# A two-layer retention, convolution and mixture-of-experts step: weight ring placed first in SBUF, other end order, token counts copied by ScalarE

## The chip, the cores and the metric

One core of a Trainium2 chip runs the whole program in one launch. The metric is the device time of one execution in microseconds (us), the median of several runs. All data is float32.

## The reference, cut to what matters

128 context tokens and 128 latent tokens pass two layers. Layer 0 mixes tokens by retention, layer 1 by a short gated convolution. After each mixer comes a layer norm and a mixture of 64 experts, of which each token uses six, and then another norm, whose result is the layer's output:

```python
x = layer_norm(DEEPNORM_ALPHA * x + g1 * y, ln_g[i, 0], ln_b[i, 0])
h = x * (1 + sc2) + sh2
y = moe_ffn(h, router_w, router_bias, w_gate, w_up, w_down, ...)
x = layer_norm(DEEPNORM_ALPHA * x + g2 * y, ln_g[i, 1], ln_b[i, 1])
```

An expert is `(silu(t @ w_gate) * (t @ w_up)) @ w_down` with weights of 1024x256, 1024x256 and 256x1024, 3 MB in all. Sixty-four experts in two layers are some 400 MB, most of what the program reads.

## The kernel before, in words

**Weights.** Every large weight passes through one SBUF tile, the ring (L37): 14 slots of 2048 floats (8 KB) per partition, 1 MB each. `plan` fixes the order of the units for the whole program; `Stream.pump` (L48) issues the next unit's DMAs on the SP queue as soon as the unit 14 places earlier is marked used (`done`), and the framework makes SP wait until the engines that read that slot are through. A gate/up unit is two DMAs of 512 KB with 4 KB per partition each (`u_gu`, L223), a down unit one of 1 MB with 8 KB per partition (`u_down`, L231). The units of the last block are loaded in column halves (`u_last`, L235): the left halves of all four experts, then the right halves.

**SBUF.** Pools are laid out in the order in which they are opened: constants (`const`), then the ring, then working tiles. In the program of before the first constant, x, lies at byte 4,224 of each partition, and the ring begins at byte 17,440, which is 34 x 512 + 32. Every ring slot is a multiple of 512 bytes long, so every slot begins 32 bytes past such a multiple.

**Routing.** `router` and `router_turn` make the scores, `route` (L1131) picks the experts. From the chosen mask (L1149) TensorE counts tokens into two PSUM banks (L1153 to L1159): `bk` holds each token's rank in its expert, `cnt` the tokens of each expert, once along the free axis (128x64) and once along the partitions (64x1). Then six small matmuls run that only keep TensorE's clock up (`warm`, L131). VectorE goes on in this order: ranks (L1164, reads `bk`), the slot tables `P0` (`slots`, L1273, four instructions), the low halves of the split activations `L` (L1169, two of 128x1024), the combine weights (L1172 to L1176), the copy of the counts out of `cnt` (L1181), sort keys (L1182, L1183; the latter reads `cnt` again), the order of the experts (L1184 to L1188).

**Gathering.** `moe` then calls `gather_first` (L1307): 32 matmuls into all four rotating PSUM banks 0 to 3, first the 16 with the high halves `H`, then 8 with `L` of the context tokens and 8 with `L` of the latent ones; inside each group bank 0 comes first and bank 3 last. `cnt` lies in one of these four banks. ScalarE copies the result to SBUF (L1316), and the first block's gate and up products (L1351) follow.

**Experts.** 24 blocks per layer (`pair`, L1406): eight of two experts, four of four, eight of two, four of four. A block multiplies gate and up in four parts (L1351), takes silu and product, turns the result (L1366), multiplies by the down weights of the block before (`down`, L1371), whose result ScalarE and VectorE split into `hi` and `lo` (L1381, L1382), and adds it to the accumulators (`combine`, L1386, matmuls of L121). VectorE takes the accumulators into the norm (`ln_part`, L982).

**The end.** In the last block (L1430 to L1446) TensorE does: down of block 22 left and right, down of block 23 left, combine of block 22 left and right, combine of block 23 left, down of block 23 right, its combine. `ln2_out` (L1541) scales and stores four tiles of 128x512: three by VectorE (L1554, L1555) and one, the right half of the context tokens, by ScalarE (L1550) and GpSimd (L1551, L1552); each goes out by a DMA of 256 KB (L1556).

`Y`, a tile of 8 KB per partition, holds the scaled norm weights first (read by GpSimd, L1002 and L1003) and later the `hi` and `lo` of every second block (L1381).

Of the kernel before, what the change touches and what calls it, by code (L numbers as in the profile page):

```python
# [7 lines left out]
F32 = mybir.dt.float32  # L8
# [3 lines left out]
AF = mybir.ActivationFunctionType  # L12
OP = mybir.AluOpType
# [4 lines left out]
NT = 2  # L18
NEXP = 64
# [52 lines left out]
class Kernel:  # L72
    WN = (12, 4, 14, 6, 22)

    def __init__(self, ctx, tc, I, O, dbg=None, nblocks=4 * len(TABLES), layers=2):
        self.ctx, self.tc, self.nc, self.I, self.O = ctx, tc, tc.nc, I, O
        self.dbg = dbg or {}
        self.nb, self.layers = nblocks, layers
        self.const = ctx.enter_context(tc.tile_pool(name="const", bufs=1))
        self.ring = ctx.enter_context(tc.tile_pool(name="ring", bufs=1))  # L80
        self.work = ctx.enter_context(tc.tile_pool(name="work", bufs=1))
        self.dram = ctx.enter_context(tc.tile_pool(name="dram", bufs=1, space=bass.MemoryType.DRAM))
        self.psum = ctx.enter_context(tc.tile_pool(name="psum", bufs=1, space=bass.MemoryType.PSUM))
        self.st = Stream(self.nc, self.ring)
        self.nm = 0
        self.pj = 0
        self.adabank = self.rtbank
        self.rt = 0
# [271 lines left out]
    def setup(self):  # L360
        nc, I, const = self.nc, self.I, self.const
        self.x = const.tile([128, NT, D], F32, name="x")
        self.cc = const.tile([128, NT, KD], F32, name="cc")
        self.st.pump(1)
        self.dummy = const.tile([128, 1], F32, name="dummy")
        self.mhalf = const.tile([128, 2], F32, name="mhalf")
        nc.gpsimd.memset(self.mhalf, -0.5)
        self.table(AF.Silu)
        self.cp = const.tile([128, 257], F32, name="cp")
        self.dl = const.tile([128, 8], F32, name="dl")  # L370
        self.t6 = self.w([128, 2 + 2 * KD + 128], F32, "T6")
        self.start_rows = self.t6[0:2 * KD, 2 + 2 * KD:]
        nc.scalar.dma_start(out=self.cp, in_=I["cst_id"])
        nc.scalar.dma_start(out=self.dl, in_=I["ret_decay"].rearrange("a d h -> a (d h)").to_broadcast([128, 8]))
        nc.sync.dma_start(out=self.cc[:, 0], in_=I["c_ctx"].rearrange("(p k) -> p k", k=KD))
        nc.sync.dma_start(out=self.cc[:, 1], in_=I["c"][0].rearrange("(p k) -> p k", k=KD))
        nc.scalar.dma_start(out=self.start_rows, in_=I["ada_b"][0, 0:2048].rearrange("(r p) -> r p", p=128))
        self.load_x()
        self.st.pump()

        self.ident, self.iota, self.part = self.cp[:, 0:128], self.cp[:, 128:256], self.cp[:, 256:257]
        self.cs = const.tile([128, 2 * KD + 32], F32, name="cs")
        nc.gpsimd.memset(self.cs, 0.0)

        self.one = const.tile([128, 3], F32, name="one")
        nc.gpsimd.memset(self.one, 0.0)
        nc.gpsimd.memset(self.one[64:128, 0:1], 1.0)
        nc.gpsimd.memset(self.one[0:64, 2:3], 1.0)
        self.gse = const.tile([128, NT, 12], F32, name="gse")
        nc.gpsimd.memset(self.gse, SENT)  # L390
        self.onesb = const.tile([128, 128], BF16, name="onesb")
        nc.gpsimd.memset(self.onesb, 1.0)
        self.trib = const.tile([128, 128], BF16, name="trib")

        self.tie = const.tile([128, NEXP + 1], F32, name="tie")
        self.rb = const.tile([128, NEXP], F32, name="rb")

        self.lnr = const.tile([128, 512], F32, name="lnr")
        nc.gpsimd.memset(self.lnr, 0.0)

        self.ab = const.tile([128, 2, KD, NT], F32, name="ab")
        self.b1, self.a1 = self.ab[:, 0], self.ab[:, 1]
        nc.scalar.activation(self.cs[:, 0:2 * KD].rearrange("p (k t) -> p k t", t=2), self.cc.rearrange("p t k -> p k t"),
                             AF.Silu)

        self.ident2 = const.tile([128, 64], F32, name="ident2")
        nc.vector.tensor_add(self.ident2, self.ident[:, 0:64], self.ident[:, 64:128])
# [413 lines left out]
    def retention(self):  # L821
        nc, U, st = self.nc, self.U, self.st
        qb, kb, bks = self.start()
        prev = None
        for h in range(4):
# [16 lines left out]
            if prev:  # L842
                z = self.ret_head_z(*prev)
# [29 lines left out]
            for d in range(2):  # L873
# [3 lines left out]
                                               op0=OP.mult, op1=OP.subtract)  # L877
            v[1] = self.w([128, 2, 512], F32R, "T6")
            if h == 1:
                for t in range(NT):  # L880
                    nc.gpsimd.tensor_scalar(self.x[:, t], self.x[:, t], ALPHA, 1.0, op0=OP.mult, op1=OP.mult)
                self.new_acc()
            if h == 2:
                for x, y in ((self.tie[:, 0:NEXP], self.iota[:, 0:NEXP]), (self.tie[:, NEXP:NEXP + 1], self.part)):
                    nc.vector.tensor_scalar(x, y, FIXED + 0.5, -2.0 ** 20, op0=OP.is_lt, op1=OP.mult)
                    nc.vector.tensor_add(x, x, y)
# [244 lines left out]
    def route(self, l):  # L1131
        nc = self.nc
# [24 lines left out]
            nc.tensor.matmul(cnt[:, 0:64], self.onesb, maskb[:, t], start=(t == 0), stop=(t == 1))  # L1157
        for t in range(NT):
            nc.tensor.matmul(cnt[0:64, 64:65], maskb[:, t], self.onesb[:, 0:1], start=(t == 0), stop=(t == 1))  # L1159
        self.warm(6)  # L1160
        V.tensor_scalar(mask, res[:, :, 0:64], HIT_T, None, op0=OP.is_ge)
        rc = self.rc = self.w([128, 2, NT, NEXP], F32, "rc")
# [11 lines left out]
        V.reciprocal(ws, ws)  # L1174
        for t in range(NT):
            V.tensor_scalar(self.comb[:, t], self.comb[:, t], ws[:, t:t + 1], 2.5, op0=OP.mult, op1=OP.mult)  # L1176

        self.od = od = self.w([128, 6, NEXP], F32, "od")
        key, self.perm, self.cnt = od[:, 0], od[0:64, 1], od[:, 2]
        kc, place = od[0:64, 3, 0:1], od[0:64, 3, 1:2]  # L1180
        V.tensor_copy(self.cnt, cnt[:, 0:64])  # L1181
        V.scalar_tensor_tensor(key, self.cnt, 64.0, self.tie[:, 0:NEXP], op0=OP.mult, op1=OP.add)  # L1182
        V.tensor_scalar(kc, cnt[0:64, 64:65], 64.0, self.tie[0:64, NEXP:NEXP + 1], op0=OP.mult, op1=OP.add)  # L1183
        V.tensor_scalar(self.perm, key[0:64], kc, None, op0=OP.is_le)  # L1184
        V.tensor_reduce(out=place, in_=self.perm, axis=AX.X, op=OP.add)
        self.above = self.w([128, NEXP], BF16, "above")
# [144 lines left out]
    def moe(self, l, fill, first):  # L1331
# [39 lines left out]
        def down(i, hT, cb, y, h, b=3):  # L1371
            bk = self.bank(b)
            us = [U["ed", l, e] for e in self.block(i)]
            m = 128 // len(us)
            for k in range(2):
                for e, u in enumerate(us):
                    w = st.get(u).rearrange("p (k c) -> p k c", k=2)
                    nc.tensor.matmul(bk[m * e:m * (e + 1)], hT[:, k, m * e:m * (e + 1)],  # L1378
                                     w[:, k, 512 * h:512 * (h + 1)], start=(k == 0), stop=(k == 1))
            hi, lo = y[h][:, 0], y[h][:, 1]  # L1380
            nc.scalar.activation(hi, bk, AF.Copy, scale=cb)  # L1381
            nc.vector.scalar_tensor_tensor(lo, bk, cb, hi.bitcast(F32), op0=OP.mult, op1=OP.subtract)  # L1382
            if h:
                st.done(*us)
# [21 lines left out]
        def pair(i):  # L1406
# [23 lines left out]
            if i == n - 1:  # L1430
                old, last = last, None
                hT2 = turn(hid)
                z = [self.w([128, 2, 512], F32R, "W", 4) for _ in range(2)]
                for h in range(2):
                    if old:
                        down(i - 1, hT, old[2], y, h, 3 - 3 * h)
                down(i, hT2, cb, z, 0)
                for h in range(2):
                    if old:
                        combine(old[1], y, h)  # L1440
                for h in range(2):
                    if h:
                        down(i, hT2, cb, z, 1, 0)
                    combine(PT, z, h)
                    for t in range(NT):
                        self.ln_part(t, h)  # L1446
# [94 lines left out]
    def ln2_out(self):  # L1541
        nc = self.nc
        g = self.g2
        mu, rs, nm = self.ln_x
        for t, h in ((0, 1), (0, 0), (1, 0), (1, 1)):
            o = self.O["y_prompt"][0] if t == 0 else self.O["y_sample"][0]
            hs = slice(512 * h, 512 * (h + 1))
            r, lg, lb = g[:, t, hs], self.lgb[0][:, hs], self.lgb[1][:, hs]
            if (t, h) == (0, 1):
                nc.scalar.activation(r, r, AF.Identity, scale=rs[t], bias=nm[t])  # L1550
                nc.gpsimd.tensor_mul(r, r, lg)  # L1551
                nc.gpsimd.tensor_add(r, r, lb)  # L1552
            else:
                nc.vector.scalar_tensor_tensor(r, r, mu[t], lg, op0=OP.add, op1=OP.mult)  # L1554
                nc.vector.scalar_tensor_tensor(r, r, rs[t], lb, op0=OP.mult, op1=OP.add)  # L1555
            (nc.scalar if (t, h) == (0, 1) else nc.sync).dma_start(out=o[:, hs], in_=r)  # L1556


    def conv_consts(self):
# [174 lines left out]
```

## Time and profile before

| | |
|---|---|
| median of 3 runs | 1453.41 us (1452.07, 1455.14, 1453.41) |
| profiled execution: its own time | 1448.27 us |
| its span, first to last instruction | 1446.5 us |
| mean granted TensorE clock | 0.963 |
| TensorE matmul busy | 1311.2 us (91%) |
| VectorE, ScalarE, GpSimd busy | 481.4, 400.5, 92.5 us |
| read from HBM | 526.49 MB |
| DMA over the span | 369 GB/s |

A busy TensorE is not one at its peak: matmuls overlap and their ends are modelled. Where a row gives a count (x10), it merges so many instructions, the first starting at the first number and all lasting together the second. A number in square brackets is how long the engine sat idle before, and which engine, tile and line released it. A granted clock of 1.00 is TensorE's 2.4 GHz, 0.50 is 1.2 GHz.

### The profile page before, as it was taken

The numbers are of one execution on the slowest core, as the hardware profiler recorded it, in microseconds if no ns is written. First come the engines' busy times: TensorE is split into PE (matmuls) and PEld (weight loads), VectorE is DVE, ScalarE is ACT, GpSimd is POOL, SyncE is SP. The second block draws the span as 40 slices with busy tenths as digits, with TensorE's granted clock in tenths as the row PEclk, the third lists the DMA queues.
The fourth block names the chain that finished last, engine by engine and source line by source line (L and its number), as shares of the span: only waits on it lengthen the run. The fifth ranks groups of instructions, "written<-read, shape, count | busy, mean of one in ns | idle before, by whom it ended". The sixth has DMA issues, their size and how long they took to land.

```text
span 1446.5 us, 21047 instructions
## 1 busy us (share of the span) xinstructions
PE 1311.2 (91%) x7558; PEld 713.0 (49%) x7558; DVE 481.4 (33%) x943; ACT 400.5 (28%) x712; POOL 92.5 (6%) x134
## 2 busy tenths in 40 slices
PE   6999999989999889998787899799999889998775
PEld 5888888644435334443221789654445224443211
DVE  4665656733121111221102866821221112121004
ACT  5654545422221012221111434322221012221001
POOL 2120110030000000000000400120000000000001
PEclk9999999999999999999999999999999999999887
DMA  9999796889999999999999999779999999999995
GB/s 289 319 394 356 264 342 242 330 335 369 408 398 410 412 411 413 413 403 399 400 357 402 341 387 400 262 248 396 394 398 412 412 401 413 412 407 413 394 379 210
DMA packets 168784, 533.24 MB, mean 369 GB/s; under 512 B 14157, under 2 KB 65541, under 8 KB 147685
## 3 DMA queue, kind: packets, MB, share of 16 engines
q1 hardware_dynamic: 165588, 527.17, 94.9%
q10 hardware_dynamic: 2768, 4.60, 0.9%
q8 instruction: 62, 1.02, 0.3%
q14 instruction: 46, 0.37, 0.1%
q0 software_dynamic: 320, 0.08, 0.0%
HBM read 526.49 MB, written 5.31 MB: 368 GB/s over the span
## 4 chain that ended last, share of the span: by engine, by line
DMA 45%; PE 42%; DVE 6%; SPq 3%; issue 2%; ACT 1%; POOL 1%; ACTq 0%; DVEq 0%; POOLq 0%
DMA ring<-in_moe_w_up 26%; DMA ring<-in_moe_w_down 14%; PE b L1351 11%; PE b L1378 6%; PE acc L121 5%; PE b L691 3%; PE b L693 3%; PE b L1301 3%; PE b L692 3%; DMA ring<-in_moe_w_gate 3%; SPq L197 2%; PE b L503 1%; DVE W L140 1%; DMA ring<-in_ada_w 1%; PE b L709 1%
## 5 line engine op out<-in xcount | busy, mean ns | idle before, releaser
L1351 PE MATMUL b<-ring,W 128*32 128x512 f32 (+1 forms) x2048 | 437.7, 628 | 57.5 <-DMA ring<-in_moe_w_up 52.7
L1382 DVE SCALAR_TENSOR_TENSOR Y<-b,cb,Y 128x512 fp32r<-128x512 f32 x92 | 69.1, 751 | 671.0 <-ACT Y L1381 671.0
L1351 PEld LDWEIGHTS b<-ring,W 128*32 128x32 f32 (+1 forms) x2048 | 104.6, 125 | 284.3 <-issue 260.9
L1378 PE MATMUL b<-ring,mtmp 128*32 128x512 f32 (+1 forms) x1024 | 222.5, 640 | 13.1 <-DMA ring<-in_moe_w_down 12.8
L1381 ACT ACTIVATE Y<-b,cb 128x512 fp32r<-128x512 f32 x92 | 63.2, 687 | 411.5 <-PE b L1378 381.0
L140 DVE TENSOR_TENSOR W<-ring,W 128x512 fp32r<-128x512 f32 x198 | 143.9, 750 | 84.6 <-ACT W L139 84.1
L139 ACT CAST W<-ring 128x512 fp32r<-128x512 f32 x197 | 117.8, 620 | 108.3 <-PE b L693 82.6
L1378 PEld LDWEIGHTS b<-ring,mtmp 128*32 128x32 f32 (+1 forms) x1024 | 57.1, 130 | 157.6 <-issue 100.5
L691 PE MATMUL b<-H,W 128*128 128x256 f32 x400 | 114.7, 287 | 2.2 <-DVE adaS L513 1.4
L693 PE MATMUL b<-H,W 128*128 128x256 f32 x400 | 113.6, 284 | 2.8 <-DVE W L140 2.8
L692 PE MATMUL b<-L,W 128*128 128x256 f32 x400 | 113.2, 283 | 0.7 <-DVE L L677 0.7
L121 PE MATMUL acc<-Y,S 128*128 128x512 f32 x368 | 100.5, 396 | 0.0
L1301 PE MATMUL b<-T,H 128*128 128x256 f32 x352 | 91.5, 293 | 6.3 <-ACT W L1305 1.4
L1301 PEld LDWEIGHTS b<-T,H 128*128 128x128 f32 x352 | 66.3, 188 | 52.2 <-PE b L1351 41.1
L1301 PE MATMUL b<-T,L 128*128 128x256 f32 x352 | 87.5, 282 | 0.0
L691 PEld LDWEIGHTS b<-H,W 128*128 128x128 f32 x400 | 76.6, 192 | 12.0 <-ACT W L139 2.5
L693 PEld LDWEIGHTS b<-H,W 128*128 128x128 f32 x400 | 76.6, 192 | 3.6 <-DVE W L140 3.4
L692 PEld LDWEIGHTS b<-L,W 128*128 128x128 f32 x400 | 76.7, 192 | 1.0 <-POOL adaS L486 0.9
L1305 ACT COPY W<-b 128x512 f32<-128x512 f32 x88 | 51.6, 586 | 84.1 <-PE b L1301 84.1
L121 PEld LDWEIGHTS acc<-Y,S 128*128 128x128 f32 x368 | 62.9, 188 | 11.9 <-issue 3.4
L1301 PEld LDWEIGHTS b<-T,L 128*128 128x128 f32 x352 | 66.7, 189 | 0.0
L1368 ACT COPY mtmp<-b 128x256 f32<-128x256 f32 x48 | 17.9, 372 | 156.5 <-PE b L1366 156.5
(331 smaller groups left out, 1297.3 us busy)
## 6 DMA issues: line engine op xcount, KB each, us to landing
ring<-in_moe_w_gate SPq DMA_DIRECT2D x256, 512.0 KB
ring<-in_moe_w_up SPq DMA_DIRECT2D x256, 512.0 KB
ring<-in_moe_w_down SPq DMA_DIRECT2D x120, 1024.0 KB
ring<-in_ada_w SPq DMA_DIRECT2D x48, 1024.0 KB
ring<-in_ret_w_in SPq DMA_DIRECT2D x20, 1024.0 KB
ring<-in_conv_w_in SPq DMA_DIRECT2D x12, 1024.0 KB
ring<-in_ret_w_out SPq DMA_DIRECT2D x8, 1024.0 KB
ring<-in_moe_w_down SPq DMA_DIRECT2D x16, 512.0 KB
```

Of the source, the lines that this page charges most:

```text
L121: self.nc.tensor.matmul(self.acc[t][h], lhsT, rhs, start=s, stop=stop, skip_group_check=True)
L139: (copy or nc.scalar.copy)(hi, src)
L140: nc.vector.tensor_sub(lo, src, hi.bitcast(F32))
L691: nc.tensor.matmul(o, hi[:, c], H[:, k], start=(k == 0), stop=False)
L692: nc.tensor.matmul(o, hi[:, c], L[:, k], start=False, stop=False)
L693: nc.tensor.matmul(o, lo[:, c], H[:, k], start=False, stop=(k == KD - 1))
L1301: nc.tensor.matmul(o, part[:, t, 128 * j:128 * (j + 1)], P[:, t, s0:s0 + 256], start=(n == 0), stop=(n == 3))
L1305: nc.scalar.copy(xg[j2 // 2][:, 2 * (j2 % 2):2 * (j2 % 2) + 2], bk.rearrange("p (c n) -> p c n", c=2))
L1351: nc.tensor.matmul(G[0][m * e:m * (e + 1)], xg[k // 4][:, k % 4, o + m * e:o + m * (e + 1)], w[:, :, k % 4], start=(k == 0), stop=(k == KD ...
L1378: nc.tensor.matmul(bk[m * e:m * (e + 1)], hT[:, k, m * e:m * (e + 1)], w[:, k, 512 * h:512 * (h + 1)], start=(k == 0), stop=(k == 1))
L1381: nc.scalar.activation(hi, bk, AF.Copy, scale=cb)
L1382: nc.vector.scalar_tensor_tensor(lo, bk, cb, hi.bitcast(F32), op0=OP.mult, op1=OP.subtract)
```

## The change

Three things. A new pool with the tile `tie`, widened from 65 to 96 floats, is opened first, and the ring's pool ahead of the constants: 4,224 + 384 = 4,608 = 9 x 512, so that the ring begins at a multiple of 512 bytes, and the constants and working tiles come behind it. In the last block the left down product of block 23 comes after the combines of block 22 and not before; in the last norm all four tiles are VectorE's, first the four products with the mean taken off, then the four that scale and shift, with the two right halves stored from the ScalarE queue. And in `route` ScalarE copies both forms of the counts out of the PSUM bank `cnt`, at once after the matmuls that make them; VectorE's sort key reads the copy.

```diff
@@ Kernel.__init__
+        self.lead = ctx.enter_context(tc.tile_pool(name="lead", bufs=1))
+        self.tie = self.lead.tile([128, 96], F32, name="tie")
+        self.ring = ctx.enter_context(tc.tile_pool(name="ring", bufs=1))
         self.const = ctx.enter_context(tc.tile_pool(name="const", bufs=1))
-        self.ring = ctx.enter_context(tc.tile_pool(name="ring", bufs=1))
@@ setup
-        self.tie = const.tile([128, NEXP + 1], F32, name="tie")
@@ route
             nc.tensor.matmul(cnt[0:64, 64:65], maskb[:, t], self.onesb[:, 0:1], start=(t == 0), stop=(t == 1))
+        self.od = od = self.w([128, 6, NEXP], F32, "od")
+        key, self.perm, self.cnt = od[:, 0], od[0:64, 1], od[:, 2]
+        kc, place = od[0:64, 3, 0:1], od[0:64, 3, 1:2]
+        nc.scalar.copy(self.cnt, cnt[:, 0:64])
+        nc.scalar.copy(kc, cnt[0:64, 64:65])
         self.warm(6)
...
-        self.od = od = self.w([128, 6, NEXP], F32, "od")
-        key, self.perm, self.cnt = od[:, 0], od[0:64, 1], od[:, 2]
-        kc, place = od[0:64, 3, 0:1], od[0:64, 3, 1:2]
-        V.tensor_copy(self.cnt, cnt[:, 0:64])
         V.scalar_tensor_tensor(key, self.cnt, 64.0, self.tie[:, 0:NEXP], op0=OP.mult, op1=OP.add)
-        V.tensor_scalar(kc, cnt[0:64, 64:65], 64.0, self.tie[0:64, NEXP:NEXP + 1], op0=OP.mult, op1=OP.add)
+        V.tensor_scalar(kc, kc, 64.0, self.tie[0:64, NEXP:NEXP + 1], op0=OP.mult, op1=OP.add)
@@ pair
-                down(i, hT2, cb, z, 0)
                 for h in range(2):
                     if old:
                         combine(old[1], y, h)
                 for h in range(2):
-                    if h:
-                        down(i, hT2, cb, z, 1, 0)
+                    down(i, hT2, cb, z, h, 3 - 3 * h)
                     combine(PT, z, h)
@@ ln2_out
-        for t, h in ((0, 1), (0, 0), (1, 0), (1, 1)):
+        parts = [(t, h) for t in range(NT) for h in range(2)]
+        cut = lambda t, h: (g[:, t, 512 * h:512 * (h + 1)], *[x[:, 512 * h:512 * (h + 1)] for x in self.lgb])
+        for t, h in parts:
+            r, lg, _ = cut(t, h)
+            nc.vector.scalar_tensor_tensor(r, r, mu[t], lg, op0=OP.add, op1=OP.mult)
+        for t, h in parts:
+            r, _, lb = cut(t, h)
+            nc.vector.scalar_tensor_tensor(r, r, rs[t], lb, op0=OP.mult, op1=OP.add)
             o = self.O["y_prompt"][0] if t == 0 else self.O["y_sample"][0]
...
-            if (t, h) == (0, 1):
-                nc.scalar.activation(r, r, AF.Identity, scale=rs[t], bias=nm[t])
-                nc.gpsimd.tensor_mul(r, r, lg)
-                nc.gpsimd.tensor_add(r, r, lb)
...
-            (nc.scalar if (t, h) == (0, 1) else nc.sync).dma_start(out=o[:, hs], in_=r)
+            (nc.scalar if h else nc.sync).dma_start(out=o[:, 512 * h:512 * (h + 1)], in_=r)
```

## Rows read from the trace of the kernel before

**Rows 1.** The page: the moved GB/s in 40 slices, and the chain by engine
```profile
GB/s 289 319 394 356 264 342 242 330 335 369 408 398 410 412 411 413 413 403 399 400 357 402 341 387 400 262 248 396 394 398 412 412 401 413 412 407 413 394 379 210
DMA 45%; PE 42%; DVE 6%; SPq 3%; issue 2%; ACT 1%; POOL 1%; ACTq 0%; DVEq 0%; POOLq 0%
```

**Rows 2.** Busy time by stretch: engines, PEclk, DMA share, GB/s; both layers' later experts
```profile
436.00:788.00 352.00, 312.71 (x1603) 124.97 (x1603) 53.95 (x99) 57.71 (x98) 1.76 (x3) 0.94 1.01 403
1078.00:1418.00 340.00, 300.65 (x1548) 120.15 (x1550) 50.45 (x91) 55.64 (x95) 0.00 (x0) 0.95 1.01 405
```

**Rows 3.** Timeline, layer 0, gather to the first expert block
```profile
291.92 1.04 PE L1313 MATMUL b<-T,H 128*128 128x256 f32 x6
292.13 2.35 DVE L1169 TENSOR_TENSOR L<-W,H 128x1024 fp32r<-128x1024 f32 x2
...
296.00 2.50 PE L1313 MATMUL b<-T,H 128*128 128x256 f32 x10 [3.04 <-DVE od L1183]
...
300.67 2.05 ACT L1316 COPY W<-b 128x512 f32<-128x512 f32 x4 [10.90 <-PE b L1313]
...
301.84 5.42 PE L1351 MATMUL b<-ring,W 128*64 128x512 f32 x24
```

**Rows 4.** Busy time by stretch, columns as rows 2, after layer 0's wait
```profile
296.00:298.00 2.00, 2.00 (x9) 2.00 (x10) 1.96 (x6) 0.00 (x0) 0.00 (x0) 0.50 1.01 420
```

**Rows 5.** Timeline, layer 1, the same place
```profile
936.57 0.94 PE L1313 MATMUL b<-T,H 128*128 128x256 f32 x6
...
940.30 2.50 PE L1313 MATMUL b<-T,H 128*128 128x256 f32 x10 [2.79 <-DVE od L1183]
...
945.12 5.44 PE L1351 MATMUL b<-ring,W 128*64 128x512 f32 x24
```

**Rows 6.** Timeline, layer 1: two neighbouring gather matmuls at the full clock
```profile
952.94 0.28 PE L1301 MATMUL b<-T,L 128*128 128x256 f32 x1
...
953.06 0.28 PE L1301 MATMUL b<-T,H 128*128 128x256 f32 x1
```

**Rows 7.** Busy time by stretch (last two numbers: DMA share, GB/s), around both gathers
```profile
304.00:308.00 4.00, 4.00 (x20) 1.24 (x18) 0.33 (x1) 0.98 (x1) 3.88 (x2) 1.00 0.36 99
...
936.00:940.00 4.00, 1.41 (x11) 1.04 (x9) 3.90 (x13) 0.00 (x0) 0.00 (x0) 1.00 0.02 4
```

**Rows 8.** Timeline, layer 0: last reader of Y, first writer of it
```profile
311.25 2.37 POOL L1003 TENSOR_TENSOR x<-x,Y 128x1024 f32<-128x1024 f32 x1
...
320.95 0.69 ACT L1381 ACTIVATE Y<-b,cb 128x512 fp32r<-128x512 f32 x1 [3.23 <-PE b L1378]
```

**Rows 9.** Busy time by stretch: spreads into other tiles, then the ring alone
```profile
918.00:928.00 10.00, 7.85 (x69) 6.13 (x67) 7.56 (x12) 3.69 (x8) 1.76 (x6) 1.00 1.02 410
...
1080.00:1100.00 20.00, 18.52 (x114) 11.87 (x110) 1.34 (x3) 3.63 (x7) 0.00 (x0) 1.00 1.02 417
1100.00:1120.00 20.00, 17.75 (x102) 11.03 (x102) 2.81 (x6) 2.50 (x4) 0.00 (x0) 1.00 1.02 411
...
1280.00:1300.00 20.00, 19.88 (x98) 8.11 (x96) 2.79 (x5) 3.93 (x7) 0.00 (x0) 1.00 1.02 402
```

**Rows 10.** Timeline, the last block
```profile
1417.92 7.32 PE L1378 MATMUL b<-ring,mtmp 128*32 128x512 f32 x42 [1.41 <-DMA ring<-in_moe_w_down]
...
1424.00 0.75 DVE L1382 SCALAR_TENSOR_TENSOR Y<-b,cb,Y 128x512 fp32r<-128x512 f32 x1 [1.09 <-ACT Y L1381]
...
1425.17 2.13 PE L121 MATMUL acc<-Y,S 128*128 128x512 f32 x8
...
1428.17 2.42 PE L1378 MATMUL b<-ring,mtmp 128*32 128x512 f32 x16
1428.68 0.14 PEld L1378 LDWEIGHTS b<-ring,mtmp 128*32 128x32 f32 x5 [0.36 <-DMA ring<-in_moe_w_down]
```

**Rows 11.** Timeline, the last norm
```profile
1435.87 0.74 DVE L1554 SCALAR_TENSOR_TENSOR G<-G,lnst,G 128x512 f32<-128x512 f32 x1
...
1441.42 1.63 DVE L1555 SCALAR_TENSOR_TENSOR G<-G,lnst,G 128x512 f32<-128x512 f32 x1
```

More of the change, by code (lines that the diff above doesn't have):

```diff
@@ L1544, in ln2_out @@
         mu, rs, nm = self.ln_x
-        for t, h in ((0, 1), (0, 0), (1, 0), (1, 1)):
-            o = self.O["y_prompt"][0] if t == 0 else self.O["y_sample"][0]
-            hs = slice(512 * h, 512 * (h + 1))
-            r, lg, lb = g[:, t, hs], self.lgb[0][:, hs], self.lgb[1][:, hs]
-            if (t, h) == (0, 1):
-                nc.scalar.activation(r, r, AF.Identity, scale=rs[t], bias=nm[t])
-                nc.gpsimd.tensor_mul(r, r, lg)
-                nc.gpsimd.tensor_add(r, r, lb)
-            else:
-                nc.vector.scalar_tensor_tensor(r, r, mu[t], lg, op0=OP.add, op1=OP.mult)
-                nc.vector.scalar_tensor_tensor(r, r, rs[t], lb, op0=OP.mult, op1=OP.add)
-            (nc.scalar if (t, h) == (0, 1) else nc.sync).dma_start(out=o[:, hs], in_=r)
+        parts = [(t, h) for t in range(NT) for h in range(2)]
[6 more added lines that the diff above has]
+            nc.vector.scalar_tensor_tensor(r, r, rs[t], lb, op0=OP.mult, op1=OP.add)
+            o = self.O["y_prompt"][0] if t == 0 else self.O["y_sample"][0]
+            (nc.scalar if h else nc.sync).dma_start(out=o[:, 512 * h:512 * (h + 1)], in_=r)
     def conv_consts(self):
```

## The prediction

> **What bounds the kernel now.** I began with the page. DMA holds 45% of the chain that ended last and TensorE 42%; from the eleventh slice on most slices move around 410 GB/s, with holes where a layer's experts begin: slices 9 and 10 (289 to 362 us) at 335 and 369, slices 26 and 27 (904 to 976 us) at 262 and 248 [rows 1]. The busy times by stretch then show what the long expert stretches wait for: the 16 DMA engines are busy throughout, at 403 and 405 GB/s, in 352 and 340 us, 692 us together [rows 2]. There a faster engine saves nothing, but whatever lets the transfers begin earlier moves the whole stretch.
>
> So I read the timeline where a layer's transfers start again, at the gather. Ring slots come free only when the first expert block has multiplied, so its start decides. In layer 0 TensorE begins the gather at 291.92, does 6 of the first 16 matmuls, which is banks 0, 1 and 2, and then sits 3.04 us until L1183 of VectorE; the block starts at 301.84 [rows 3]. L1183 is the last reader of the bank of the counts, here the fourth of the gather's banks; the slot tables and `H`, which these matmuls need, were ready long before. Behind the wait the granted clock stands at 0.50, the lower level of 1.2 GHz [rows 4]. Layer 1 shows the same: 6 matmuls at 936.57, a wait of 2.79 us, the block at 945.12 [rows 5].
>
> **The counts copied by ScalarE.** Removed from VectorE is one copy of 128x64, which lies behind the slot tables and `L` and ahead of nothing that will then be late. Added are two small copies on ScalarE right behind the count matmuls. ScalarE has been idle 10.90 us when it takes the gather's result [rows 3], so they cost nothing and hold up nothing; no DMA is issued from its queue there. If ScalarE were busy, the same bank would come free later by what it is doing. What they do is to free the fourth bank before TensorE arrives at it, and the wait goes.
>
> What is late next is `L`: its two subtractions start at 292.13 and last 2.35 us [rows 3], so the halves are there at about 293.3 and 294.5. At the full clock gather matmuls follow each other in 0.12 us [rows 6]. Then the 16 with `H` end at 291.92 + 16 x 0.12 = 293.8, the first 8 with `L` at 294.8, and the last 8 at 295.8, each behind its operand. ScalarE's first copy out (2.05 us for four [rows 3], so about 0.5) ends before that, since bank 0 is complete first, and the block starts at about 295.9 in place of 301.84: **5.9 us** earlier. Of these 3.0 are the wait and the rest the half clock behind it. In layer 1 the same gives 936.57 + 32 x 0.12 = 940.4, the block at 940.5 in place of 945.12: **4.6 us**. The lower end of both is the wait alone, 3.0 + 2.8 = 5.8 us, if the clock fell for another reason; the upper end is 10.5. I take 10.5, because the six matmuls ahead of the wait in layer 1 ran at that pace too: 0.94 us [rows 5] is 5 x 0.12 and the 0.28 of the last [rows 6].
>
> Does the saving reach the end? In layer 1 the DMA engines stand idle before the block (share 0.02 at 936 to 940), so transfers start 4.6 us earlier. In layer 0 they are still draining the ring up to 304 and then idle (0.36 of 304 to 308 [rows 7]). Against 411 GB/s the two slices from 289 to 362 us lose (411 - 335) / 411 x 36 = 6.7 and (411 - 369) / 411 x 36 = 3.7 us [rows 1]. That is more than 5.9, so an earlier release of slots can be used in full: it fills these holes. From there on the transfers run without a pause, and the convolution behind layer 0 starts when its experts end. One thing doesn't move: GpSimd reads `Y` until 311.25 + 2.37 = 313.6, and the first write of it by ScalarE, now at 320.95 [rows 8], comes to 315.0. That leaves 1.4 us, so no new wait.
>
> **The order in the last block.** From 1417.92 TensorE runs 42 down matmuls, the last 16 of them block 23's left half, then 8 and 4 matmuls of the combines (2.13 us the 8), and block 23's right half from 1428.17 in 2.42, of which 0.36 waits for its weights [rows 10]. So a half takes 2.06 us, and the left one began at 1423.2. In the new order the combines of block 22 come at 1423.2; their last operand is ready at 1424.00 + 0.75 = 1424.75, so they end at about 1425.3. Block 23's left half runs to 1427.4, its `hi` and `lo` need 0.69 [rows 8] and 0.75 us [rows 10], and its combine ends at about 1429.5; only then comes the right half, with its weights landed: 1431.5 in place of 1430.6. That is **+0.9 us**: the combines of block 22 used to cover the split, and now TensorE stands still through it. At the least it is nothing, at the most the 1.45 of the split.
>
> **The last norm.** VectorE's first step starts at 1435.87 and lasts 0.74; its last one now ends at 1441.42 + 1.63 = 1443.05 [rows 11]. Eight steps of 0.76 in a row end at 1441.95, and the scale that the second four need is computed beside the first four. The last step takes 0.76 and not 1.63, since GpSimd, which worked on the fourth tile beside it, has nothing left to do. **-1.1 us**, with 0 and -1.6 as ends. Two stores move to the ScalarE queue, one more than before; nothing else is left on that engine, and the last of them leaves as soon as the SP one would have. No ring unit is left to issue here, so SP holds nothing back.
>
> **The ring's place.** Every ring slot moves from 32 bytes past a multiple of 512 to such a multiple. No row shows a load to such an address. The nearest are loads elsewhere: the norm weights and gates spread into `Y` and `G`, tiles that lie at other offsets, are among the transfers of 918 to 928, which move 410 GB/s, where the ring alone moves 411; its best and worst stretches of 20 us are at 417 and 402 [rows 9]. By these a gain is at most 6 / 411 of 692 us = 10 us and a loss at most 9 / 411 = 15 us. I take **0**, the row of the other tiles being nearest.
>
> **Sum.** -5.9 - 4.6 + 0.9 - 1.1 + 0 = -10.7 us. The profiled execution took 1448.27 us, so 1437.6; it was 5.1 us below the median of the runs, 1453.41, and from the median the sum gives 1442.7. I say 1442.7.
>
> **The rivals.**
>
> - *The ring's rows get cheaper.* Gate and up rows are 4 KB, two thirds of an expert's bytes, down rows 8 KB. A row that begins 32 bytes past a boundary ends in a piece of its own of 32 bytes. If that piece costs its share, 32 in 4,128 and 32 in 8,224, the weighted saving is 0.65% of 692 us = 4.5 us, and the time 1438.2; up to the 10 us above, 1432.7. For it: DMA is the bound there. Against it: tiles at other offsets move no slower and no faster. Chance 0.20. The Trainium skill, "DMA: Bandwidth & Descriptors", section "How a descriptor splits into AXI transactions", says that a transfer which doesn't start at a multiple of 256 bytes has its first transaction start at the boundary below and spends beats on bytes that nobody uses. By that rule the 4.5 us would come; the rows of the trace neither show nor exclude it, as every slot has the same offset.
> - *Layer 0's share is hidden.* Its transfers drain until 304 whether TensorE starts at 296 or 302. If what limits them afterwards is not the release of slots, layer 0 gives nothing and 1442.7 + 5.9 = 1448.6 remains. Against it stand the 6.7 and 3.7 us of holes. Chance 0.10.
> - *The wait only changes its owner.* If the fourth bank is held by something else up to the same place, or the framework still makes the gather wait for VectorE's sort keys, TensorE stands as long as now and only the end of the kernel is left: -0.2 us, 1453.2. For it: the row names only the last releaser. Against it: all that the gather reads was there 3 us earlier. Chance 0.07. That the ring doesn't land on a multiple of 512 would be part of the forecast, where its place costs nothing.
> - *Slower: the aligned ring loads at a lower rate.* All slots, the constants and the working tiles change place. If the 692 us ran at 402 GB/s as in the worst stretch and not at 411, they would cost 15 us more, and the time would be 1458. It decides from a loss of 10.7 / 692 = 1.5% on. For it: rates of 402 do occur. Against it: they occur with unchanged addresses. Chance 0.05.
>
> The forecast keeps 0.58.
>
> **How the numbers follow.** The likeliest case gives 1442.7, by the bounds of its terms from 1441 to 1448. The range reaches down into the first rival, to 1432, and up past the second, to 1450: 0.58 + 0.10 + most of 0.20 is some 0.84. About 0.2%, 2.9 us, is what a measurement of this kernel can tell from no change, its three runs being 3.1 us apart. Faster by more than that are the forecast, the first rival and most of the second: 0.87. Within it lies the third, with the rest of the second: 0.08. Slower 0.05.
>
> **What would show it.** Right: in both layers 32 gather matmuls with no wait on L1183, the clock at 1.00 through them, the first block 4.0 us behind the first gather matmul, where it now comes 9.9 and 8.6 us behind it; the first slots released that much earlier; DMA rate in the later experts as before; TensorE idle in the last block during the split of block 23's left half; eight equal steps in the norm. Wrong: a gather that waits again, the first block earlier but the experts of layer 0 ending at the same time, or 20 us stretches of the ring steadily off 411 GB/s.

## The result, and the profile after

The changed kernel took 1425.85 us (median of 5, 1423.71 to 1435.38) against 1453.41: ratio 0.9837 [0.9813, 0.986], which is 23.7 us less [20.3, 27.2]. Run a second time, beside other executions of before, it took 1430.34 us, ratio 0.9869 [0.9833, 0.9905]. So the same program's medians can lie 4.5 us apart, and smaller differences below are not settled by medians. The forecast was 1442.7, its range 1432 to 1450: the right sign and less than half the size.

Two readings come first. The gather runs as forecast. Here is the timeline of the kernel after around it, layer 0 and then layer 1, answering to [rows 3, 5]:

```profile
287.06 0.21 ACT L1166 COPY od<-b 128x64 f32<-128x64 f32 x1 [0.90 <-PE b L1161]
...
287.17 0.15 ACT L1167 COPY od<-b 64x1 f32<-64x1 f32 x1
...
288.31 2.24 PE L1316 MATMUL b<-T,H 128*128 128x256 f32 x16
...
288.52 2.35 DVE L1177 TENSOR_TENSOR L<-W,H 128x1024 fp32r<-128x1024 f32 x2
...
290.39 2.08 PE L1316 MATMUL b<-T,L 128*128 128x256 f32 x16
...
292.43 0.72 PE L1354 MATMUL b<-ring,W 128*64 128x512 f32 x2
...
926.32 2.15 PE L1316 MATMUL b<-T,H 128*128 128x256 f32 x16
...
928.31 2.08 PE L1316 MATMUL b<-T,L 128*128 128x256 f32 x16
...
930.35 0.72 PE L1354 MATMUL b<-ring,W 128*64 128x512 f32 x2
```

ScalarE has freed the bank at 287.32, 1.0 us before the gather begins; no wait is left, and the first block follows the first gather matmul by 4.1 and 4.0 us. The granted clock through it, busy time by stretch (last three numbers: clock, DMA share, GB/s), against 0.50 in [rows 4]:

```profile
288.00:290.00 2.00, 2.00 (x18) 1.98 (x18) 2.00 (x4) 0.00 (x0) 0.00 (x0) 1.00 1.06 434
290.00:292.00 2.00, 2.00 (x19) 2.00 (x18) 1.93 (x10) 0.21 (x1) 0.00 (x0) 1.00 1.00 420
```

But the rate of the ring didn't stay. The same view, before:

```profile
436.00:476.00 40.00, 36.53 (x222) 22.10 (x223) 5.26 (x10) 6.82 (x12) 0.00 (x0) 1.00 1.02 413
...
1100.00:1140.00 40.00, 32.15 (x178) 14.22 (x182) 5.19 (x10) 3.56 (x6) 0.00 (x0) 0.94 1.02 410
```

and after:

```profile
436.00:476.00 40.00, 35.49 (x214) 20.78 (x216) 4.84 (x9) 5.03 (x10) 0.00 (x0) 1.00 1.02 420
...
1100.00:1140.00 40.00, 34.48 (x166) 13.57 (x168) 4.84 (x9) 3.56 (x6) 0.00 (x0) 0.91 1.02 422
```

The DMA engines are full in both, share about 1.02, and move 420 to 422 GB/s where they moved 410 to 413. No slice of before's page is above 413 from the eleventh on [rows 1]; the page after has 418, 422, 421:

```profile
GB/s 317 352 390 348 249 331 244 343 341 382 401 393 418 422 415 386 402 403 404 417 364 412 361 407 403 235 317 399 396 400 416 421 408 401 401 393 387 393 375 233
```

The profiled execution of after happens to be the slowest of its five (1435.38 us, span 1433.6), so its total says little; its stretches do.

### The profile page after: what moved, and what is told of

It is laid out like the page before. It is cut to its first block, busy times and chain, and to the rows that moved or that the text cites. A ratio compares the mean times of both kernels' runs of the same rounds, so it can differ in the third digit from the quotient of the medians.

```text
span 1433.6 us, 21046 instructions
## 1 busy us (share of the span) xinstructions
PE 1309.4 (91%) x7558; PEld 711.4 (50%) x7558; DVE 481.2 (34%) x943; ACT 400.0 (28%) x715; POOL 88.1 (6%) x132
## 2 busy tenths in 40 slices
DMA packets 168784, 533.24 MB, mean 372 GB/s; under 512 B 14157, under 2 KB 65541, under 8 KB 147685
## 3 DMA queue, kind: packets, MB, share of 16 engines
q8 instruction: 62, 1.02, 0.3%
## 4 chain that ended last, share of the span: by engine, by line
PE 54%; DMA 36%; DVE 5%; issue 2%; ACT 1%; SPq 1%; POOL 0%; DVEq 0%; ACTq 0%; POOLq 0%
DMA ring<-in_moe_w_up 21%; PE b L1354 15%; DMA ring<-in_moe_w_down 11%; PE b L1381 7%; PE acc L124 7%; PE b L1304 4%; PE b L692 3%; PE b L694 3%; PE b L693 3%; DMA ring<-in_moe_w_gate 2%; PE b L504 1%; DVE W L143 1%; PE b L605 1%; PE b L710 1%; PE b L709 1%
## 5 line engine op out<-in xcount | busy, mean ns | idle before, releaser
L1354 PE MATMUL b<-ring,W 128*32 128x512 f32 (+1 forms) x2048 | 445.9, 633 | 55.9 <-DMA ring<-in_moe_w_up 51.8
L1354 PEld LDWEIGHTS b<-ring,W 128*32 128x32 f32 (+1 forms) x2048 | 108.0, 125 | 287.4 <-issue 267.1
L1381 PE MATMUL b<-ring,mtmp 128*32 128x512 f32 (+1 forms) x1024 | 217.9, 624 | 12.5 <-DMA ring<-in_moe_w_down 12.5
```

Source lines behind the costliest of these rows:

```text
L1354: nc.tensor.matmul(G[0][m * e:m * (e + 1)], xg[k // 4][:, k % 4, o + m * e:o + m * (e + 1)], w[:, :, k % 4], start=(k == 0), stop=(k == KD ...
```

## The experiments

Kernels are named by what they have. Each is set against executions of before on the same chip; a gain in us is (1 - ratio) x 1453.41, its interval likewise.

**One part alone.** `ring_only` is before with the two pools moved:

```diff
+        self.lead = ctx.enter_context(tc.tile_pool(name="lead", bufs=1))
+        self.tie = self.lead.tile([128, 96], F32, name="tie")
+        self.ring = ctx.enter_context(tc.tile_pool(name="ring", bufs=1))
         self.const = ctx.enter_context(tc.tile_pool(name="const", bufs=1))
-        self.ring = ctx.enter_context(tc.tile_pool(name="ring", bufs=1))
...
-        self.tie = const.tile([128, NEXP + 1], F32, name="tie")
```

> The kernel before with the ring's place alone changed. Theory A, each row that lands in the ring costs less time at a multiple of 512: 13 to 18 us faster than before, the stretches that wait for transfers at 417 to 422 GB/s where before shows 411. Theory B, the place is worth nothing and all of the gain comes from the earlier gather: within 3 us of before, 411 GB/s as before.

Measured 1440.0 us, 0.9926 [0.9899, 0.9953]: **-10.8 us** [-14.7, -6.8]. Theory A has the rate; its 13 to 18 us lie mostly above the interval. The rates of the changed kernel are here:

```profile
436.00:476.00 40.00, 36.91 (x229) 21.14 (x230) 4.84 (x9) 5.09 (x10) 0.00 (x0) 1.00 1.02 420
...
1100.00:1140.00 40.00, 35.16 (x176) 14.08 (x174) 4.84 (x9) 3.56 (x6) 0.00 (x0) 0.91 1.02 421
```

`counts_only` is before with the change's lines in `route`:

```diff
+        nc.scalar.copy(self.cnt, cnt[:, 0:64])
+        nc.scalar.copy(kc, cnt[0:64, 64:65])
...
-        V.tensor_copy(self.cnt, cnt[:, 0:64])
...
```

> The kernel before with the counts copied by ScalarE alone. Theory A: the block 4.1 us behind the first gather matmul in both layers, 9 to 10.5 us faster in all, or 5 to 7 if layer 0 gives some of it back in a new wait of TensorE on VectorE and GpSimd, as the trace of after has it near 305. Theory B: some 24 us faster, the whole gain.

1443.53 us, 0.9945 [0.9925, 0.9964]: **-8.0 us** [-10.9, -5.2]; 413 GB/s at 436 to 476 us. `end_only` is before with the last block's order and the last norm:

```diff
-                down(i, hT2, cb, z, 0)
...
+                    down(i, hT2, cb, z, h, 3 - 3 * h)
...
```

> The kernel before with the last block's order and the last norm alone changed. Both theories: within 1.5 us of before, the right half's down about 0.9 us later, the norm about 1 us shorter.

1450.25 us, 0.9986 [0.9968, 1.0004]: -2.0 us, not told apart from nothing. The three sum to -20.8, between the two measurements of the whole.

**Is it the address, or the order of the pools?** `off32` is the changed kernel with every slot 32 bytes on:

```diff
-        self.tie = self.lead.tile([128, 96], F32, name="tie")
+        self.tie = self.lead.tile([128, 104], F32, name="tie")
```

> The kernel after with 32 bytes more ahead of the ring, so that it begins 32 bytes past a multiple of 512 as before, while the pools keep their new order. Theory A: 13 to 18 us slower than after, that is 6 to 10 us faster than before, 411 GB/s. Theory B, and also if the new place of the constants and working tiles made the gain: as fast as after, some 24 us faster than before.

1438.6 us, 0.9917 [0.9894, 0.9941]: by the ratios 32 bytes take back 11.6 us against the first measurement of the changed kernel and 7.0 against the second, less than the 13 to 18 expected, and the rate is that of before. The 32 bytes move every tile behind the ring too, but in the two stretches read here every transfer issued goes into the ring. So it is the address, and the ring's.

**Which multiple?** The same line with 112, 128 and 160 columns puts the slots 64, 128 and 256 bytes past a multiple of 512 (`off64`, `off128`, `off256`).

> The kernel after with the ring 64 bytes past a multiple of 512. Theory C, a row pays when it begins off a multiple of 64: as fast as after, 420 GB/s and more in the stretches of the four-expert blocks. Theory D, it pays off a multiple of 256 or 512, as the page has it for 256: as the ring at 32, about 12 us slower than after, 411 GB/s.

> The kernel after with the ring 128 bytes past a multiple of 512. Theory C: as fast as after, 420 GB/s and more. Theory D: about 12 us slower than after, 411 GB/s. A third possibility, a cost in steps, would put it between the ring at 64 and the one at 0.

> The changed kernel with 160 columns in the tile ahead of the ring in place of 96, so that all 65 slots begin 256 bytes past a multiple of 512; nothing else differs. Theory E, a start at any multiple of 256 is as good as one of 512 (what the rule of the pages would say): as fast as the changed kernel, about 1426 us, 420 to 422 GB/s at 436 to 516 us and at 1100 to 1160. Theory F, it takes a multiple of 512: as the rings at 32, 64 and 128 past it, 1438 to 1440 us, 411 to 414 GB/s there. In both the gather stays without a wait, the first block 4 to 5 us behind the first gather matmul.

1439.21 [0.9876, 0.9943], 1439.3 [0.9887, 0.9948] and 1429.63 us [0.9825, 0.9885]. The busy time by stretch once more, of `off32`:

```profile
1100.00:1140.00 40.00, 33.93 (x170) 15.66 (x170) 4.84 (x9) 4.15 (x7) 0.00 (x0) 0.91 1.02 413
```

of `off64`:

```profile
1100.00:1140.00 40.00, 34.40 (x174) 15.94 (x173) 4.84 (x9) 4.15 (x7) 0.00 (x0) 0.91 1.02 412
```

of `off128`:

```profile
1100.00:1140.00 40.00, 34.54 (x211) 17.70 (x204) 6.88 (x13) 6.06 (x10) 0.00 (x0) 1.00 1.02 413
```

and of `off256`:

```profile
1100.00:1140.00 40.00, 33.64 (x179) 11.94 (x176) 2.84 (x6) 3.94 (x7) 0.00 (x0) 0.91 1.02 421
```

(The text on `off256` speaks of 65 slots; the ring has 14.) A multiple of 256 is what counts; 64 and 128 are as bad as 32. My theory that 64 would do fell, and 512 asks for more than is needed.

**The changed kernel once more**, on the chip of `off256`:

> The changed kernel itself once more, beside the ring at 256 bytes past a multiple of 512. Every theory: about 1426 us, 420 to 422 GB/s at 436 to 516 us. Open is whether the 2.4 us pause of VectorE behind the first block of layer 0, which stands in its first profile and not in that of the ring at 32 bytes past, comes again: if it belongs to the change, block 1 begins some 15 us behind block 0 again; if it was that one execution's, 13 us or less.

1430.34 us, so as fast as `off256`. The pause of VectorE came again, at the same instruction:

```profile
304.19 2.34 POOL L1005 TENSOR_TENSOR x<-x,Y 128x1024 f32<-128x1024 f32 x1
304.20 2.41 DVE L1211 TENSOR_TENSOR od<-od 128x64 f32<-128x64 f32 x1
```

against the timeline of `off256`, where VectorE comes first:

```profile
304.17 0.23 DVE L1211 TENSOR_TENSOR od<-od 128x64 f32<-128x64 f32 x1
304.20 2.41 POOL L1005 TENSOR_TENSOR x<-x,Y 128x1024 f32<-128x1024 f32 x1
```

0.01 us behind GpSimd's product VectorE's small subtraction lasts as long as that product; 0.03 us ahead of it, it lasts 0.23. Other profiled executions lie between: in `ring_only`, `end_only`, `off64`, `counts_only`, `best`, `after_oldorder` and `off128` the subtraction starts inside a product, takes 0.47 to 1.64 us, and each time ends 0.08 us behind that product's end.

**A subtraction with one operand in PSUM.** `one_operand` is the changed kernel with

```diff
-        V.tensor_scalar(a, bk[:, 0:64], FIXED + 0.5, CAP / 2, op0=OP.is_ge, op1=OP.mult)
-        V.tensor_scalar(b, bk[:, 0:64], FIXED + FEW + 0.5, CAP / 2, op0=OP.is_ge, op1=OP.mult)
-        V.tensor_sub(self.od[:, 4], a, b)
+        V.tensor_scalar(b, bk[:, 0:64], FIXED + FEW + 0.5, 1.0, op0=OP.is_ge, op1=OP.mult)
+        V.scalar_tensor_tensor(a, bk[:, 0:64], FIXED + 0.5, b, op0=OP.is_ge, op1=OP.subtract)
```

and the factor `CAP / 2` in the two additions that use the result.

> The changed kernel with the subtraction of the slot order written so that one of its operands is the PSUM bank itself (one instruction fewer; the factor 32 moves into the two additions that use it). Theory G, the 2.40 us of that subtraction in layer 0 are VectorE held off by GpSimd's product, which reads two SBUF tiles, begun 0.02 us earlier: with a PSUM operand it takes 0.2 to 0.3 us whatever GpSimd does, block 1 of layer 0 begins 13.1 us behind block 0 and not 15.3 to 15.8, and layer 0's last down matmul comes some 4 us earlier; median 1422 to 1426. Theory H, VectorE was late for another reason (an operand, a queue): the pause moves to the neighbouring instruction, block 1 still 15 us or more behind.

1426.5 us, 0.9823 [0.98, 0.9846]. Its timeline:

```profile
302.86 2.38 POOL L1004 TENSOR_TENSOR x<-G,Y 128x1024 f32<-128x1024 f32 x1
...
304.75 0.23 DVE L1210 SCALAR_TENSOR_TENSOR od<-b,od 128x64 f32<-128x64 f32 x1
```

In the middle of a GpSimd product it takes 0.23 us, and block 1 comes 13.0 us behind block 0, not 15.3 or 15.8. `best2`, further down, has the same subtraction and the same again: 0.22 us inside a product, and 13.0 us. The new operation itself isn't what frees it: before, in the last norm, the same SCALAR_TENSOR_TENSOR with its tiles in SBUF takes 0.74 us alone and 1.63 when it starts inside a product of GpSimd [rows 11], whose row is

```profile
1440.91 1.59 POOL L1552 TENSOR_TENSOR G<-G,G 128x512 f32<-128x512 f32 x1
```

Theory G holds for the wait. The total, 1426.5, is at the upper end of its 1422 to 1426 and lies within what two medians of the changed kernel differ by, so the 4 us forecast at this place are not shown in the end time.

**Better than both?** `after_oldorder` is the changed kernel with the old order of the last block:

```diff
+                down(i, hT2, cb, z, 0)
...
-                    down(i, hT2, cb, z, h, 3 - 3 * h)
+                    if h:
+                        down(i, hT2, cb, z, 1, 0)
```

> The kernel after with the old order in the last block, so that block 23's left down comes ahead of the combines of block 22. If the stall behind the split of the left half is what the new order costs: 0.9 us faster than after, visible in the rows of the last block, less than the runs can tell. If the left half's weights come late, nothing.

1426.38 us, 0.9829 [0.9801, 0.9858]. `best` adds that the four transposes of the next layer's modulation rows (PE L566, behind the pause) go to the second block,

```diff
-        s = self.ada_sum(1, 0, range(4, 8), self.ada_bk)
-        self.ada_cols(self.ada_cols_T(s, self.bank(3)))
+        self.ada_s = self.ada_sum(1, 0, range(4, 8), self.ada_bk)
...
+    def ada_turn(self):
+        self.ada_cols(self.ada_cols_T(self.ada_s, self.bank(3)))
...
```

and `best2` has the old order with `one_operand`'s subtraction:

> The kernel after with the old order in the last block, and with the four transposes of the modulation rows, which make TensorE wait in layer 0 for VectorE beside GpSimd, put one block later. If that wait takes back a part of what the counts gave in layer 0: 3 to 5 us faster than after. If it was a matter of one execution: within 2 us of after.

> The same edit and the old order of the last block (block 23's left half ahead of block 22's combines), as the candidate to beat both kernels. By the runs so far the order is worth at most 1 to 2 us. Theory G: 1421 to 1425, block 1 of layer 0 some 13.1 us behind block 0. Theory H: 1426 as the changed kernel with the old order.

1426.6 us, 0.9828 [0.9802, 0.9855], and 1427.91 us, 0.9817 [0.9788, 0.9847]. None is told apart from the changed kernel; all beat before by as much. Neither the 3 to 5 us hoped for from `best` is shown, nor the 1421 to 1425 of theory G for `best2`.

## Why the prediction was wrong

**The step that failed is "The ring's place", taken as 0.** It measured -10.8 us [-14.7, -6.8], as large as the whole forecast, and just past the bound of 10 that I had drawn from the ring's best 20 us. I chose 0 because "tiles at other offsets" moved 410 GB/s [rows 9]. They were no other case: x lies at byte 4,224, 128 past a multiple of 256, and in the program of before `Y` begins at 156,736 and the first `G` at 142,368, 64 and 32 past. `off64` and `off128` show that such starts are as slow as 32. A comparison in which nothing is aligned can't price alignment. With -10.8 in place of 0 the sum is -21.5 us, inside the intervals of both measurements of the whole. The range missed for the same reason: its lower end was that term at its bound, with nothing left for the others to be off.

**The first rival** (chance 0.20) had the direction, and both its factors wrong. Its 0.65% per row is too small. The two stretches give 420 / 413, 1.7%, and 421 / 410, 2.7%, and they mix rows of 4 and 8 KB differently. The traces also hold each packet's time, a packet being one such row. Taken over 436 to 788 and 1078 to 1400 us, the median packet of 4 KB took 162 ns in `before` and `off32` and 159 in `ring_only`, `after` and `off256`; one of 8 KB took 313 against 309. On the rings at a multiple of 256 the 10th and the 90th percentile are 159 and 309 as well; before they are 159 and 166, 309 and 320. So a row that begins 32 bytes past costs some 3 to 4 ns, whether it is long or short. With two thirds of the bytes in 4 KB rows that is 1.7%, where the rival's 32 bytes in 4,128 would be 1.2 ns. The piece is no packet of its own: the pages of `before` and `after` count 168784 packets each.

Its 692 us aren't all paced by DMA. The spans of the profiled executions, cut at the starts of the first matmuls of gathers and blocks and of the last down matmul of each layer (us):

| stretch | before | ring_only | counts_only | off32 | off256 | after | after again |
|---|---|---|---|---|---|---|---|
| start to gather, layer 0 | 291.9 | 288.5 | 291.9 | 292.6 | 288.4 | 288.3 | 288.4 |
| gather to block | 9.9 | 7.4 | 4.1 | 4.1 | 4.1 | 4.1 | 4.1 |
| experts, layer 0 | 488.2 | 483.1 | 488.7 | 486.9 | 483.1 | 490.3 | 491.6 |
| to gather, layer 1 | 146.6 | 144.4 | 145.4 | 146.4 | 144.2 | 143.6 | 144.3 |
| gather to block | 8.5 | 7.0 | 4.0 | 5.0 | 4.0 | 4.0 | 4.0 |
| experts, layer 1 | 484.9 | 484.1 | 494.5 | 487.9 | 485.3 | 488.5 | 480.4 |
| end | 16.5 | 16.5 | 16.5 | 14.8 | 14.7 | 14.7 | 14.8 |

1.7% of 692 us would be 12 us; the experts of `ring_only` gave 5.1 + 0.8, and the stretches ahead of the gathers 3.4 + 2.2. In the blocks of two experts TensorE sets the pace. The timeline shows the same matmuls of two neighbouring blocks, before:

```profile
558.01 1.94 PE L1351 MATMUL b<-ring,W 128*64 128x512 f32 x8
...
573.75 1.51 PE L1351 MATMUL b<-ring,W 128*64 128x512 f32 x6
```

and in `ring_only`:

```profile
550.70 1.94 PE L1352 MATMUL b<-ring,W 128*64 128x512 f32 x8
...
566.44 1.94 PE L1352 MATMUL b<-ring,W 128*64 128x512 f32 x8
```

Both are 15.74 us apart, and in neither is a matmul's wait put down to a transfer between 540 and 650 us. Two experts of 3.15 MB in 15.74 us need 400 GB/s, less than either rate: a faster ring fills up and then waits for slots. The busy share in [rows 2] doesn't tell the two apart. In `ring_only` it hardly falls when, inside the same eight blocks, the rate drops to what TensorE takes; and the long stretch of layer 0 rose only from 403 to 408 GB/s, 1.2%. The busy time by stretch:

```profile
580.00:620.00 40.00, 39.77 (x196) 17.29 (x196) 6.69 (x12) 8.47 (x16) 0.00 (x0) 1.00 1.02 422
...
620.00:660.00 40.00, 39.65 (x197) 17.59 (x194) 10.78 (x19) 9.38 (x16) 0.00 (x0) 1.00 1.01 401
...
436.00:788.00 352.00, 310.88 (x1602) 124.08 (x1601) 59.49 (x111) 59.03 (x101) 4.23 (x10) 0.94 1.01 408
```

Layer 1's 480.4 to 494.5 also show how far one stretch varies between executions, so the table is for where, not for sizes.

The Trainium skill's rule on which that rival leaned ("DMA: Bandwidth & Descriptors", "How a descriptor splits into AXI transactions": a start off a multiple of 256 costs beats) agrees with the runs on the multiple, 421 GB/s at 256 and 412 to 413 below. The section speaks of bytes that are fetched; what moved here is where they land. It doesn't agree on the size: by an estimate from its beats of 32 bytes, bytes below the start would cost 1, 2 and 4 beats in a 4 KB row's 128 at offsets 32, 64 and 128, and the runs show the same rate for all three.

**The counts.** The place and the mechanism were right: 4.1 and 4.0 us for a forecast of 4.0, -5.8 and -4.5 us in the trace for -5.9 and -4.6. The end time gave -8.0 [-10.9, -5.2], an interval that holds the forecast of -10.5. (The pace I read from [rows 5] was a little short: 5 x 0.12 + 0.28 is 0.88, not 0.94. The changed kernel's 16 matmuls with `H` take 2.24 and 2.15 us, 0.13 apart.) Of its parts, the wait is sure and the half clock is not: in `ring_only`, with the wait still there, the ten matmuls behind it ran at the full clock, 1.46 us for the 2.50 of [rows 3]:

```profile
292.59 1.46 PE L1314 MATMUL b<-T,H 128*128 128x256 f32 x10 [3.03 <-DVE od L1184]
```

Why it fell in one and not in the other is open, and so is whether the 2.5 + 1.5 us that `ring_only`'s gathers took less in that execution belong to the -10.8; the changed kernel against `off32`, neither with a wait at its gather, gave 7.0 to 11.6 us for the place. In `off32` the first 16 matmuls of layer 1's gather took 3.17 us, at a clock of 0.50 from 930 to 932 us, with no wait inside the gather; TensorE had stood idle for 1.88 us up to 927.46. So the clock can be at its lower level there without the wait on the counts.

"From there on the transfers run without a pause" was wrong for the changed kernel. The third rival itself fell, as no wait is left at the gather; but its idea, a wait that changes its owner, had a share one block later. With the block 5.8 us earlier, VectorE's subtraction moved from the end of GpSimd's work, where it took 0.22 us, into it. The timeline of the kernel after shows it:

```profile
304.06 2.34 POOL L1005 TENSOR_TENSOR x<-x,Y 128x1024 f32<-128x1024 f32 x1
304.08 2.40 DVE L1211 TENSOR_TENSOR od<-od 128x64 f32<-128x64 f32 x1
...
306.40 0.68 DVE L519 TENSOR_TENSOR adaS<-acc,adaS 128x512 f32<-128x512 f32 x1
...
307.18 0.63 PE L566 MATMUL b<-cp,adaS 128*128 128x128 f32 x4 [2.73 <-issue]
...
307.74 3.63 PE L1354 MATMUL b<-ring,W 128*64 128x512 f32 x8
```

and its busy time by stretch, what follows:

```profile
308.00:312.00 4.00, 4.00 (x12) 0.86 (x10) 0.10 (x2) 0.18 (x1) 3.05 (x2) 0.59 0.51 207
312.00:316.00 4.00, 4.00 (x20) 1.29 (x18) 0.00 (x0) 0.77 (x2) 0.00 (x0) 1.00 0.31 94
```

TensorE stands 2.73 us ahead of the transposes of L519's result, its clock falls (0.59 over these 4 us), eight matmuls take 3.63 us for 1.94, slots come free late, and the DMA engines idle. `one_operand` has shares of 0.91 and 0.97 in these two stretches. Block 2 comes 33.8 us behind block 0 here and 33.7 in the second measurement, 29.9 in `before` and `off256`: so 3.8 to 3.9 of layer 0's 5.8 us are lost again when the subtraction falls at the start of a GpSimd product.

**The end.** The order cost what was said: TensorE stands through block 23's split, 1413.15 + 1.92 to 1415.88, and from the end of block 22's down products to the end of block 23's it takes 1410.85 to 1417.33 + 2.14, 8.6 us, where [rows 10] give 1423.2 to 1428.17 + 2.42, 7.4. So it is +1.2 for a forecast of +0.9. The timeline of the kernel after:

```profile
1410.85 2.37 PE L124 MATMUL acc<-Y,S 128*128 128x512 f32 x8
...
1413.15 1.92 PE L1381 MATMUL b<-ring,mtmp 128*32 128x512 f32 x16
...
1415.88 1.52 PE L124 MATMUL acc<-W,S 128*128 128x512 f32 x4 [0.81 <-ACT W L1384]
...
1417.33 2.14 PE L1381 MATMUL b<-ring,mtmp 128*32 128x512 f32 x16
...
1424.74 2.81 DVE L1550 SCALAR_TENSOR_TENSOR G<-G,lnst,G 128x512 f32<-128x512 f32 x4
...
1427.47 2.73 DVE L1553 SCALAR_TENSOR_TENSOR G<-G,lnst,G 128x512 f32<-128x512 f32 x4
```

The norm's eight steps take 1424.74 to 1430.20, 5.5 us for the 6.1 forecast, as neighbouring steps overlap by 0.07; before it was 7.2 [rows 11]. That is -1.7 for -1.1. Together -0.5 for -0.2, and `end_only` can't tell it from nothing.

The rival that layer 0's share is hidden falls by `counts_only`: there layer 0's last down matmul starts at 291.9 + 4.1 + 488.7 = 784.7 us for 790.0 before, so in that execution 5.3 of the 5.8 us reach the end of the layer. In the changed kernel a part went to the new pause. The slower rival found nothing: at 436 to 476 and 1100 to 1140 us every ring at a multiple of 256 moved 417 GB/s or more, every other 414 or less.

## What to carry to other kernels

Start an SBUF tile that large transfers fill at a multiple of 256 bytes: here, for a ring with rows of 4 and 8 KB, that was some 2% of rate, and the pools' order decides it. Before pricing such a thing from neighbours, ask whether any neighbour has the property. And DMA engines that look busy throughout need not set the pace: compare the bytes of a block over its period with the rate, since a gain in rate pays only where the first is not already the smaller.

## What the runs showed that I had not expected

- Starts 32, 64 and 128 bytes past a multiple of 256 cost the same: at 436 to 476 and 1100 to 1140 us such rings moved 410 to 414 GB/s, those at 0 and 256 417 to 422, in rows of 4 and 8 KB. At 32 bytes the median row costs 3 to 4 ns more, the short one as the long one; at 128 the median 4 KB row is at 159 ns too, and the slowest tenth take 169 or more in place of 159.
- A VectorE subtraction of two SBUF tiles of 128x64 takes 0.23 us, or up to 2.41 when it starts inside a GpSimd product of 128x1024 from SBUF, since it then ends 0.08 us behind that product; with one operand in PSUM it takes 0.23 beside the same product. The Trainium skill, "SBUF — State Buffer", "SBUF: two separate sides", says that a VectorE operation with two SBUF inputs and a GpSimd one that reads SBUF share a port pair which whoever comes first holds for a whole instruction; the traces agree, 2.40 and 2.41 us behind against 0.23 ahead.
